# A new first stage for a hybrid decoder layer: another way to spread silu(c), sums of squares as columns, whole modulation tiles, another order of loads

## The chip, the core and the metric

The kernel runs on one core of one Trainium2 chip. Times are device microseconds of one execution. The kernel before takes 1126.01 us, the median of 3 runs (1125.87 to 1126.14).

The engines are named as in the profile: PE is TensorE (matrix products; PEld is its loading of weights), DVE is VectorE, ACT is ScalarE, SP is SyncE, which here only issues DMAs. Each engine works through its own queue in order.

## The reference

One decoder layer on 512 tokens of 1024 features. A vector c gives six modulation vectors; two of them, a shift and a scale, modulate the first norm. The normed rows h then go through one wide input projection (q, k, v, gates and the inputs of the other mixers), three mixers, an output projection, and an MLP behind a second norm.

```
cond = jax.nn.silu(c)
...
mod = (cond @ w_ada[l] + b_ada[l])[:, None, :]
sh1, sc1, g1, sh2, sc2, g2 = jnp.split(mod, 6, axis=-1)
h = _rms(x, norm1_w[l]) * (1 + sc1) + sh1
x = x + g1 * _hybrid_mixer(h, w_in[l], ...)
h = _rms(x, norm2_w[l]) * (1 + sc2) + sh2
x = x + g2 * (jnp.square(jax.nn.relu(h @ w_ff1[l])) @ w_ff2[l])
```

with `_rms(x, w) = x * rsqrt(mean(x * x) + eps) * w` over the features of a token. Everything is float32.

## The kernel before

Activations lie transposed: a block is [128 features, 512 tokens], and `xT` has eight of them. Weights are split into a high and a low part as they stream in, and a product is three fp32r matmuls (`mm3`, L284 to L287): high weight by low activation, high by high, low by high. Large products are fed by `wstream` (L274), which loads two row blocks of 512 columns into a tile `raw`, and `wsplit` (L267), which lets ACT make `wh` and DVE make `wl`. Each of the three has a pool of three buffers. Other tiles of [128, 512] come from 59 places, taken in the order in which they have been free (`Slots`).

The first stage, L330 to L486, stands in an order written out by hand for DVE, ACT, PE and SP (`manual_schedule`). It makes h and the first two chunks of the input projection, Q and K, as the modulation arrives:

- c is loaded twice in halves, spread over all 128 partitions by the DMA (L334); ACT makes silu of it in place (`crow`, L356).
- `warm(n)` (L390) is n products of 128x128 ones by ones. They feed nothing; they keep PE working. `WARM = (18, 12, 6)`.
- Squares of the eight `xT` blocks: ACT squares, DVE adds pairs (L403), and PE sums over features with a 128x128 matrix of ones (L401, L404) into `sp` [128, 512]: every partition has the sum of every token.
- DVE picks the diagonals of `sp` (L414, tile diag), so that token sums stand in a column, `ss` [128, 4]. ACT takes the square root (L416), DVE the reciprocal and one Newton step (L421 to L424).
- `diag` times ones (L428, L429) spreads 1/rms back over the partitions, tile `rp` (psrx in the profile).
- `ada_load` (L226) loads 128 rows of w_ada^T in two halves, tiles `wa`; `dot` (L362) multiplies a half by silu(c) and sums it, `dot_end` (L369) joins two halves with bias and norm weight into `A1[k]` (scale and shift of row block k).
- `high(k)` and `low(k)` (L439, L448) make the two parts `hh[k]` and `hl[k]` of h from x, 1/rms and A1; `w_load`, `w_high`, `w_low` load and split the weights of Q and K for a row block. For row block 0, `u` (L445) reads `rp` in PSUM.
- The loop of L462 runs over the eight row blocks: the loads, dots and splits of block k + 1 beside PE's 24 matmuls of block k.

Behind it a scheduler orders the work by priority; `evac` (L316) takes finished products out of PSUM, and `background` holds the other 32 modulation rows (`ada_later`, L241), one per two row blocks.

Of the kernel before, what the change touches and what calls it, by code (L numbers as in the profile page):

```python
# [17 lines left out]
P = 128  # L18
D = 1024
T = 512  # L20
# [65 lines left out]
# columns of the vector table: 128 values each  # L86
# [7 lines left out]
# chunks of 512 columns of w_in  # L94
# [4 lines left out]
def kernel(ctx: ExitStack, tc: tile.TileContext, a: dict, out: bass.AP, dbg=None):  # L99
# [16 lines left out]
    class Slots:  # L116
        """places of [128, 512] float32: the one that has been free for longest goes first"""
# [56 lines left out]
    crow = [blk("crow") for _ in range(2)]  # L174
# [8 lines left out]
    # 1/sqrt(sum/n + eps) of a small tile of sums  # L183
# [10 lines left out]
    def token_rsqrt(sums, n, name):  # L194
        """1/sqrt(sum over the partitions of sums / n + eps) on every partition, in PSUM"""
        nb = sums.shape[1] // P
        sp = psm(name)
        for b in range(nb):
            mm(sp[:, b : b + 1], lhsT=sums[:, b * P : (b + 1) * P], rhs=ones[:, 0:1], start=True, stop=True)
        ss = small([P, 4], name, 2)[:, :nb]  # L200
        V.tensor_copy(ss, sp[:, :nb])
        free(sp)
        return spread(rsqrt_small(ss, n, name + str(nb)), nb, name)

    def spread(r, nb, name):
        """columns of tokens to rows, the same on every partition, in PSUM"""
# [25 lines left out]
    def ada_dot(wa, o):  # L232
        d = small([P, 2], "dot", 4)
        for i in range(2):
            V.scalar_tensor_tensor(wa[i], wa[i], 1.0, crow[i], ALU.mult, ALU.mult, accum_out=d[:, i : i + 1])  # L235
# [12 lines left out]
    # work beside the large products: handed out one piece per two row blocks of weights  # L248
# [3 lines left out]
    def tick(n=1):  # L252
# [4 lines left out]
        if ticks[0] % 2 == 0 and background:  # L257
            background.pop(0)()
            if not background:
                free(*crow)  # L260
# [28 lines left out]
    def gemm_feat(w, nk, ch, ah, al, k0=0):  # L289
        """4 blocks [128 columns of w, 512 tokens]"""  # L290
# [10 lines left out]
    def gemm_tok(w, nk, ch, ah, al, mod, ahead=None):  # L301
        """4 blocks [128 tokens, 512 columns of w]; tokens 128 b + p, or 4 p + b with mod"""
# [13 lines left out]
    def evac(ps, name, func=AF.Copy):  # L316
        """out of PSUM, ahead of other work"""
# [13 lines left out]
    E = mybir.EngineType  # L331
    with tc.manual_schedule(engines={E.DVE, E.Activation, E.PE, E.SP}):
        for i in range(2):
            nc.sync.dma_start(crow[i], a["c"][:, i * T : (i + 1) * T].broadcast_to([P, T]))  # L334
# [6 lines left out]

        for k in range(8):
            nc.sync.dma_start(xT[k], a["x"][k])
            if k == 0:
                nc.sync.dma_start(vec, a["vec"])
            if k == 1:
                nc.sync.dma_start(cst[:, :P], a["const"][:, :P])
        wa = [ada_load(1, 0)]
        wa.append(ada_load(0, 0))
# [5 lines left out]
        for i in range(2):  # L355
            S.activation(crow[i], crow[i], AF.Silu)  # L356
        S.activation(junk1, epsc, AF.Sqrt)
        A1 = [small([P, 2], f"A1{k}") for k in range(8)]
        bsc1 = small([P, 8], "bsc1")
        dots = {}  # L360

        def dot(k, i, half):  # L362
            if (k, i) not in dots:
                dots[k, i] = small([P, 2], "dot", 4)
            x = wa[i][half]
            V.scalar_tensor_tensor(x, x, 1.0, crow[half], ALU.mult, ALU.mult, accum_out=dots[k, i][:, half : half + 1])  # L366
            free(x)

        def dot_end(k, i):  # L369
            d, o = dots[k, i], A1[k][:, i : i + 1]  # L370
            if i == 0:
                V.scalar_tensor_tensor(o, d[:, 0:1], bsc1[:, k : k + 1], d[:, 1:2], ALU.add, ALU.add)
                V.tensor_tensor(o, o, vc("norm1_w", k), ALU.mult)
            else:
                V.scalar_tensor_tensor(o, d[:, 0:1], vc("b_ada", k), d[:, 1:2], ALU.add, ALU.add)
# [18 lines left out]
        warm(WARM[0])  # L394
        sp = psm("sx")
        for k in range(0, 8, 2):
            s0, s1 = blk("sq"), blk("sq")
            S.activation(s0, xT[k], AF.Square)
            S.activation(s1, xT[k + 1], AF.Square)
            if k == 6:  # L400
                mm(sp, lhsT=ones, rhs=s0, start=False, stop=False)  # L401
            else:
                V.tensor_tensor(s1, s0, s1, ALU.add)  # L403
            mm(sp, lhsT=ones, rhs=s1, start=(k == 0), stop=(k == 6))  # L404
            free(s0, s1)
            if k == 0:
                V.tensor_scalar(bsc1, vc("b_ada", 8, 8), 1.0, None, ALU.add)
        dot(0, 0, 0)
        dot(0, 0, 1)
        dot_end(0, 0)  # L410
        ss, var, rt, r, t = (small([P, 4], "rx" + n) for n in "svryt")
        dg = [small([P, P], f"diag{b}") for b in range(4)]
        for b in range(4):
            V.scalar_tensor_tensor(dg[b], sp[:, b * P : (b + 1) * P], 1.0, ident, ALU.mult, ALU.mult, accum_out=ss[:, b : b + 1])  # L414
        free(sp)
        S.activation(rt, ss, AF.Sqrt, scale=1.0 / D, bias=epsc)  # L416
        w_high(Q, 0)
        w_high(K, 0)
        V.tensor_scalar(var, ss, 1.0 / D, EPS, ALU.mult, ALU.add)
        dot(0, 1, 0)  # L420
        V.reciprocal(r, rt)  # L421
        V.tensor_tensor(t, r, r, ALU.mult)
        V.scalar_tensor_tensor(t, t, -0.5, var, ALU.mult, ALU.mult)
        V.scalar_tensor_tensor(r, t, 1.5, r, ALU.add, ALU.mult)  # L424
        warm(WARM[1])
# [849 lines left out]
```

## Time and profile before

| | |
|---|---|
| median of 3 runs | 1126.01 us |
| the profiled execution: span | 1123.5 us |
| busy in it: PE, DVE, ACT | 1116.0, 597.9, 492.2 us |
| instructions | 14055 |
| data read from HBM | 131.41 MB, 119 GB/s over the span |

The profile has one execution. A row of its timeline is the start in us from the start of the span, the length, the engine, the line, the operation with its tiles (out<-in), its shape and xcount, and in brackets the idle time ahead of it with what ended that. Buffer numbers are left out of the tile names. A row of a table by stages is a stretch, its length, the busy time (and instructions) of PE, PEld, DVE, ACT and POOL, the granted clock of PE, the DMA share and GB/s. A grouped row ends in the busy time, the mean ns of one instruction, and the idle time ahead of the group.

### The profile page before, as it was taken

How to read it: one execution, taken by the hardware profiler on the slowest of the kernel's cores; microseconds unless marked ns; L12 is line 12 of the kernel's file. 1: busy time of each engine (PE TensorE's matmuls, PEld its weight loads, DVE VectorE, ACT ScalarE, POOL GpSimd, SP SyncE). 2: the span in 40 equal slices, each digit the busy share in tenths (PEclk: the TensorE clock that was granted, in tenths of full speed). 3: DMA queues.
4: the chain of work that ended last, by engine and by line, in shares of the span. 5: the costliest groups of instructions: out<-in, count | busy, mean ns of one | idle time of the engine just before them, and what ended most of it. 6: DMA issues, size and time to landing. Idle time of an engine off the chain costs nothing.

```text
span 1123.5 us, 14055 instructions
## 1 busy us (share of the span) xinstructions
PE 1116.0 (99%) x5414; PEld 952.2 (85%) x5414; DVE 597.9 (53%) x1210; ACT 492.2 (44%) x937; POOL 0.2 (0%) x4
## 2 busy tenths in 40 slices
PE   8999999999999999999999999999999999999998
PEld 6889998999887888888888888899888888888887
DVE  6973763572667668468833424576354233445241
ACT  5475885543497448425432123353343111344120
POOL 0000000000000000000000000000000000000000
PEclk9999999999999999999999999999999999999999
DMA  9852253333543444322333422360122233322331
GB/s 342 299 183 98 96 164 105 105 104 130 166 135 103 132 142 131 115 83 75 104 113 104 159 94 94 115 204 1 57 93 94 95 101 103 96 95 94 94 131 38
DMA packets 49347, 134.45 MB, mean 120 GB/s; under 512 B 5616, under 2 KB 6384, under 8 KB 49280
## 3 DMA queue, kind: packets, MB, share of 16 engines
q1 hardware_dynamic: 47696, 130.81, 35.6%
q10 hardware_dynamic: 1584, 2.75, 0.8%
q8 instruction: 42, 0.69, 0.2%
q14 instruction: 25, 0.20, 0.1%
HBM read 131.41 MB, written 2.13 MB: 119 GB/s over the span
## 4 chain that ended last, share of the span: by engine, by line
PE 95%; ACT 2%; DVE 2%; DMA 1%; issue 0%; SPq 0%; DVEq 0%; ACTq 0%
PE psacc L285 29%; PE psacc L287 29%; PE psacc L286 29%; PE psS L555 1%; PE psy L867 1%; PE pso L671 1%; PE psyo L875 1%; PE pso L669 1%; DVE conv L786 0%; PE pskT L539 0%; PE psqT L534 0%; PE pspT L652 0%; DVE wa L366 0%; PE psst L827 0%; DMA crow<-in_c_dram 0%; PE pssx L404 0%
## 5 line engine op out<-in xcount | busy, mean ns | idle before, releaser
L271 DVE TENSOR_TENSOR wl<-raw,wh 128x1024 fp32r<-128x1024 f32 x161 | 196.9, 1223 | 348.1 <-ACT wh L270 346.4
L270 ACT CAST wh<-raw 128x1024 fp32r<-128x1024 f32 x161 | 168.9, 1050 | 378.4 <-PE psacc L286 326.2
L285 PE MATMUL psacc<-hl,wh 128*128 128x512 f32 x416 | 168.0, 404 | 0.7 <-ACT prev L830 0.6
L287 PE MATMUL psacc<-hh,wl 128*128 128x512 f32 x416 | 163.2, 392 | 0.0
L286 PE MATMUL psacc<-hh,wh 128*128 128x512 f32 x416 | 162.1, 390 | 0.0
L285 PEld LDWEIGHTS psacc<-hl,wh 128*128 128x128 f32 x416 | 78.3, 188 | 18.0 <-issue 1.2
L287 PEld LDWEIGHTS psacc<-hh,wl 128*128 128x128 f32 x416 | 78.1, 188 | 18.2
L285 PE MATMUL psacc<-wl,hh 128*128 128x512 f32 x224 | 93.4, 419 | 0.0
L286 PEld LDWEIGHTS psacc<-hh,wh 128*128 128x128 f32 x416 | 78.2, 188 | 17.7 <-issue 1.4
L285 PE MATMUL psacc<-al,wh 128*128 128x512 f32 (+1 forms) x242 | 92.1, 381 | 0.0
L286 PE MATMUL psacc<-ah,wh 128*128 128x512 f32 (+1 forms) x242 | 92.1, 381 | 0.0
L287 PE MATMUL psacc<-ah,wl 128*128 128x512 f32 (+1 forms) x242 | 92.1, 380 | 0.0
L286 PE MATMUL psacc<-wh,hh 128*128 128x512 f32 x224 | 90.1, 402 | 0.0
L287 PE MATMUL psacc<-wh,hl 128*128 128x512 f32 x224 | 89.7, 401 | 0.0
L285 PE MATMUL psacc<-gl,wh 128*128 128x512 f32 x224 | 88.3, 394 | 0.0
L287 PE MATMUL psacc<-gh,wl 128*128 128x512 f32 x224 | 87.6, 392 | 0.0
L286 PE MATMUL psacc<-gh,wh 128*128 128x512 f32 x224 | 86.9, 388 | 0.0
L286 PEld LDWEIGHTS psacc<-wh,hh 128*128 128x128 f32 x224 | 65.9, 294 | 1.4
L285 PEld LDWEIGHTS psacc<-wl,hh 128*128 128x128 f32 x224 | 65.5, 293 | 1.7
L287 PEld LDWEIGHTS psacc<-wh,hl 128*128 128x128 f32 x224 | 65.5, 293 | 1.5
L235 DVE SCALAR_TENSOR_TENSOR wa<-wa,crow 128x512 f32<-128x512 f32 x64 | 43.5, 686 | 21.4 <-DMA wa<-in_w_ada_dram 21.3
L285 PEld LDWEIGHTS psacc<-al,wh 128*128 128x128 f32 x242 | 45.5, 188 | 8.9
(342 smaller groups left out, 1914.4 us busy)
## 6 DMA issues: line engine op xcount, KB each, us to landing
raw<-in_w_in_dram SPq DMA_DIRECT2D x80, 512.0 KB, 3.5
raw<-in_w_ff_dram SPq DMA_DIRECT2D x64, 512.0 KB, 3.5
wa<-in_w_ada_dram SPq DMA_DIRECT2D x96, 256.0 KB, 4.6
wst<-in_w_in_dram SPq DMA_DIRECT2D x16, 256.0 KB, 5.4
M<-prow SPq DMA_DIRECT2D x16, 256.0 KB, 3.4
raw<-in_w_ssd_out_dram SPq DMA_DIRECT2D x8, 512.0 KB, 3.5
raw<-in_w_pool_out_dram SPq DMA_DIRECT2D x8, 512.0 KB, 3.4
raw<-in_w_out_dram SPq DMA_DIRECT2D x8, 512.0 KB, 3.4
```

The source lines that it names most:

```text
L235: V.scalar_tensor_tensor(wa[i], wa[i], 1.0, crow[i], ALU.mult, ALU.mult, accum_out=d[:, i : i + 1])
L270: S.copy(wh, raw)
L271: V.tensor_tensor(wl, raw, wh.bitcast(F32), ALU.subtract)
L285: mm(ps, lhsT=wh, rhs=xl, start=first, stop=False)
L286: mm(ps, lhsT=wh, rhs=xh, start=False, stop=False)
L287: mm(ps, lhsT=wl, rhs=xh, start=False, stop=last)
L555: mm(so[b], lhsT=qT[:, b * P : (b + 1) * P], rhs=kT[:, (b + 1) * P - n : (b + 1) * P], start=True, stop=True)
L669: mm(od, lhsT=vs[kb][:, hs], rhs=pT[b // 2][:, cs : cs + P], start=(b == 0), stop=False, skip_group_check=True)
L671: mm(ov[:, b, :], lhsT=vs[b][:, hs], rhs=pT[0][:, b * P : (b + 1) * P], start=False, stop=(gi == 2 and b == 3), skip_group_check=True)
L867: mm(yp[half * 64 : half * 64 + 64, cs], lhsT=X[c][:, (2 * j + half) * 64 : (2 * j + half + 1) * 64], rhs=Ms[half][:, cs], start=True, sto ...
L875: mm(op[:, cs], lhsT=prev[c][:, j * P : (j + 1) * P], rhs=CT[:, cs], start=True, stop=True)
```

## The change

All of it lies in the first stage (but for `crow`, which is now one tile of its own that isn't given back, and so is read as `crow[:, i, :]` by the later dots).

- c is loaded as two rows of one partition, on ACT's DMA queue, together with the vector table and the identity. ACT makes silu of the row; PE spreads it over the partitions as a product of a row of ones with it, into two PSUM banks; DVE copies each into `crow`.
- The sums of squares: `square_sums` takes the squares as the stationary operand and one column of ones as the moving one, four products of 128x1 per call, so that token sums come out as columns. The diagonal step is gone. The last pair of squares isn't added by DVE: ACT squares one, DVE the other, and PE sums both. Behind each of the four pairs stand four `warm` products.
- A row block of w_ada is one load of 512 KB and one `dot` over 1024 elements; A1 needs one small step instead of two or one of three operands. Its tiles live in turn in the buffers of `raw`, `wh` and `wl`.
- SP's loads: the first w_ada tile goes ahead of x, the second behind it.

```diff
-    crow = [blk("crow") for _ in range(2)]
+    crow = cpool.tile([P, 2, T], F32, name="crow")
...
+        c1 = [blk("c1") for _ in range(2)]
         for i in range(2):
-            nc.sync.dma_start(crow[i], a["c"][:, i * T : (i + 1) * T].broadcast_to([P, T]))
+            nc.scalar.dma_start(c1[i][:1], a["c"][:, i * T : (i + 1) * T])
+        nc.scalar.dma_start(vec, a["vec"])
+        nc.scalar.dma_start(cst[:, :P], a["const"][:, :P])
...
+        homes = [(raws, "raw"), (wsp, "wh"), (wsp, "wl")]
+
+        def ada_whole(part, k):
+            pool, tag = homes[0]
+            homes.append(homes.pop(0))
+            w = pool.tile([P, 2, T], F32, tag=tag, name=uid("wada"))
+            nc.sync.dma_start(w, a["w_ada"][part * 8 + k].rearrange("p (i t) -> p i t", i=2))
+            return w
+
+        wa = [ada_whole(1, 0)]
         for k in range(8):
             nc.sync.dma_start(xT[k], a["x"][k])
...
-        wa = [ada_load(1, 0)]
-        wa.append(ada_load(0, 0))
+        wa.append(ada_whole(0, 0))
...
+        def dot(k, i):
+            w, o, d = wa[i], A1[k][:, i : i + 1], small([P, 1], "dot1", 4)
+            V.scalar_tensor_tensor(w, w, 1.0, crow, ALU.mult, ALU.mult, accum_out=d)
             if i == 0:
-                V.scalar_tensor_tensor(o, d[:, 0:1], bsc1[:, k : k + 1], d[:, 1:2], ALU.add, ALU.add)
-                V.tensor_tensor(o, o, vc("norm1_w", k), ALU.mult)
+                V.scalar_tensor_tensor(o, d, bsc1[:, k : k + 1], vc("norm1_w", k), ALU.add, ALU.mult)
             else:
-                V.scalar_tensor_tensor(o, d[:, 0:1], vc("b_ada", k), d[:, 1:2], ALU.add, ALU.add)
+                V.tensor_tensor(o, d, vc("b_ada", k), ALU.add)
...
         warm(WARM[0])
+        cps = [psm("c") for _ in range(2)]
+        for i in range(2):
+            S.activation(c1[i][:1], c1[i][:1], AF.Silu)
+            mm(cps[i], lhsT=ones[:1], rhs=c1[i][:1], start=True, stop=True)
+            V.tensor_copy(crow[:, i, :], cps[i])
+        free(*cps, *c1)
+        S.activation(junk1, epsc, AF.Sqrt)
+        V.tensor_scalar(bsc1, vc("b_ada", 8, 8), 1.0, None, ALU.add)
+
         sp = psm("sx")
+
+        def square_sums(s, first, last):
+            for b in range(4):
+                mm(sp[:, b : b + 1], lhsT=s[:, b * P : (b + 1) * P], rhs=ones[:, 0:1], start=first and b == 0, stop=last and b == 3, skip_group_check=True)
+
         for k in range(0, 8, 2):
             s0, s1 = blk("sq"), blk("sq")
             S.activation(s0, xT[k], AF.Square)
-            S.activation(s1, xT[k + 1], AF.Square)
-            if k == 6:
-                mm(sp, lhsT=ones, rhs=s0, start=False, stop=False)
+            if k < 6:
+                S.activation(s1, xT[k + 1], AF.Square)
+                V.tensor_tensor(s1, s0, s1, ALU.add)
             else:
-                V.tensor_tensor(s1, s0, s1, ALU.add)
-            mm(sp, lhsT=ones, rhs=s1, start=(k == 0), stop=(k == 6))
+                square_sums(s0, False, False)
+                V.tensor_tensor(s1, xT[k + 1], xT[k + 1], ALU.mult)
+            square_sums(s1, k == 0, k == 6)
             free(s0, s1)
-            if k == 0:
-                V.tensor_scalar(bsc1, vc("b_ada", 8, 8), 1.0, None, ALU.add)
-        dot(0, 0, 0)
-        dot(0, 0, 1)
-        dot_end(0, 0)
...
-        for b in range(4):
-            V.scalar_tensor_tensor(dg[b], sp[:, b * P : (b + 1) * P], 1.0, ident, ALU.mult, ALU.mult, accum_out=ss[:, b : b + 1])
...
+            warm(4)
+            if k == 2:
+                dot(0, 0)
+        dot(0, 1)
+        v, r, t, rt = (small([P, 4], "rx" + n) for n in ("v", "r", "t", "rt"))
+        S.activation(rt, sp[:, :4], AF.Sqrt, scale=1.0 / D, bias=epsc)
+        V.tensor_scalar(v, sp[:, :4], 1.0 / D, EPS, ALU.mult, ALU.add)
...
-                wa = [ada_load(1, k + 1), ada_load(0, k + 1)]
+                wa = [ada_whole(1, k + 1), ada_whole(0, k + 1)]
                 w_load(k + 1)
-                dot(k + 1, 0, 0)
+                dot(k + 1, 0)
                 if k:
                     low(k)
-                dot(k + 1, 0, 1)
                 w_high(Q, k + 1)
                 w_high(K, k + 1)
-                dot(k + 1, 1, 0)
-                dot_end(k + 1, 0)
-                dot(k + 1, 1, 1)
+                dot(k + 1, 1)
                 w_low(Q, k + 1)
-                dot_end(k + 1, 1)
```

The chain from `rt` to `diag` and `rp`, and `warm(WARM[1])` and `warm(WARM[2])` around it, stay as they were.

PE's queue from its start to the spreading of 1/rms, before (lines of the kernel before; pswarm is the tile of the warm products, pssx the sums of squares, psrx the spread 1/rms; the moving operand stands first behind the arrow):

```order
L392 MATMUL pswarm_134<-ones_87 128x128 x18
L404 MATMUL pssx_153<-sq_155,ones_87 128x512
L404 MATMUL pssx_153<-sq_162,ones_87 128x512
L404 MATMUL pssx_153<-sq_168,ones_87 128x512
L401 MATMUL pssx_153<-sq_173,ones_87 128x512
L404 MATMUL pssx_153<-sq_174,ones_87 128x512
L392 MATMUL pswarm_134<-ones_87 128x128 x12
L429 MATMUL psrx_223<-diag_49_189,ones_87 128x128
```

The same place in the changed kernel (its own line numbers; psc is silu(c) spread):

```order
L389 MATMUL pswarm_128<-ones_86 128x128 x18
L395 MATMUL psc_147<-c_15_93,ones_86 128x512
L395 MATMUL psc_148<-c_16_94,ones_86 128x512
L405 MATMUL pssx_157<-ones_86,sq_159 128x1 x4
L389 MATMUL pswarm_128<-ones_86 128x128 x4
L405 MATMUL pssx_157<-ones_86,sq_172 128x1 x4
L389 MATMUL pswarm_128<-ones_86 128x128 x4
L405 MATMUL pssx_157<-ones_86,sq_188 128x1 x4
L389 MATMUL pswarm_128<-ones_86 128x128 x4
L405 MATMUL pssx_157<-ones_86,sq_200 128x1 x4
L405 MATMUL pssx_157<-ones_86,sq_201 128x1 x4
L389 MATMUL pswarm_128<-ones_86 128x128 x16
```

The spread of c stands between the first warm products and the sums, and the warm products ahead of psrx are 16 in a row, with 12 more between the sums.

DVE's queue at the same place, before, from the first sum of squares to the first dot:

```order
L403 TENSOR_TENSOR sq_155<-sq_154,sq_155 128x512
L407 TENSOR_SCALAR bsc_32_133<-vec_76 128x8
L403 TENSOR_TENSOR sq_162<-sq_161,sq_162 128x512
L403 TENSOR_TENSOR sq_168<-sq_167,sq_168 128x512
L366 SCALAR_TENSOR_TENSOR wa_106,dot_179<-wa_106,crow_77 128x512
L366 SCALAR_TENSOR_TENSOR wa_107,dot_179<-wa_107,crow_78 128x512
```

And in the changed kernel, from the copies of `crow`:

```order
L396 COPY crow<-psc_147 128x512
L396 COPY crow<-psc_148 128x512
L399 TENSOR_SCALAR bsc_30_127<-vec_76 128x8
L412 TENSOR_TENSOR sq_159<-sq_158,sq_159 128x512
L412 TENSOR_TENSOR sq_172<-sq_171,sq_172 128x512
L368 SCALAR_TENSOR_TENSOR wada_99,dot_39_184<-wada_99,crow 128x1024
L370 SCALAR_TENSOR_TENSOR A_22_119<-dot_39_184,bsc_30_127,vec_76 128x1
L412 TENSOR_TENSOR sq_188<-sq_187,sq_188 128x512
L415 TENSOR_TENSOR sq_201<-xT_9_85 128x512
L368 SCALAR_TENSOR_TENSOR wada_109,dot_44_216<-wada_109,crow 128x1024
```

The two copies out of PSUM now stand ahead of the first sum of squares, and the first whole dot ahead of the third.

SP's queue just behind the stage in the changed kernel (raw: weights of the third chunk, two row blocks each; wa: background modulation rows); the third `raw` there stood right behind the first two `wa` before:

```order
L276 DMA raw_796<-in_w_in_dram 128x1024
L713 DMA hv_88<-in_hvec_dram 128x48
L718 DMA wdt_829<-in_w_dt_dram 128x128
L276 DMA raw_834<-in_w_in_dram 128x1024
L229 DMA wa_883<-in_w_ada_dram 128x512
L229 DMA wa_884<-in_w_ada_dram 128x512
L229 DMA wa_998<-in_w_ada_dram 128x512
L229 DMA wa_999<-in_w_ada_dram 128x512
L229 DMA wa_1149<-in_w_ada_dram 128x512
L229 DMA wa_1150<-in_w_ada_dram 128x512
L276 DMA raw_892<-in_w_in_dram 128x1024
```

The third `raw` has moved behind four more background loads.

More of the change, by code (lines that the diff above doesn't have):

```diff
@@ L234, in ada_dot @@
         for i in range(2):
-            V.scalar_tensor_tensor(wa[i], wa[i], 1.0, crow[i], ALU.mult, ALU.mult, accum_out=d[:, i : i + 1])
+            V.scalar_tensor_tensor(wa[i], wa[i], 1.0, crow[:, i, :], ALU.mult, ALU.mult, accum_out=d[:, i : i + 1])
         free(*wa)
@@ L258, in tick @@
             background.pop(0)()
-            if not background:
-                free(*crow)
     def flush():
@@ L398 @@
             S.activation(s0, xT[k], AF.Square)
[L399 to L404 removed]
+            if k < 6:
+                S.activation(s1, xT[k + 1], AF.Square)
+                V.tensor_tensor(s1, s0, s1, ALU.add)
+            else:
+                square_sums(s0, False, False)
+                V.tensor_tensor(s1, xT[k + 1], xT[k + 1], ALU.mult)
+            square_sums(s1, k == 0, k == 6)
             free(s0, s1)
[L406 to L416 removed]
+            warm(4)
[5 more added lines that the diff above has]
+        V.tensor_scalar(v, sp[:, :4], 1.0 / D, EPS, ALU.mult, ALU.add)
         w_high(Q, 0)
         w_high(K, 0)
[L419 to L420 removed]
         V.reciprocal(r, rt)
         V.tensor_tensor(t, r, r, ALU.mult)
[L423 removed]
+        V.scalar_tensor_tensor(t, t, -0.5, v, ALU.mult, ALU.mult)
         V.scalar_tensor_tensor(r, t, 1.5, r, ALU.add, ALU.mult)
+        free(sp)
         warm(WARM[1])
         rp = psm("rx")
+        dg = [small([P, P], f"diag{b}") for b in range(4)]
         for b in range(4):
@@ L431 @@
         R1 = blk("R1")
-        dot(0, 1, 1)
-        dot_end(0, 1)
         hh = [cpool.tile([P, T], F32R, name=f"hh{k}", tag=f"hh{k}") for k in range(8)]
```

15 lines of the change are left out of this document (removed).

## The prediction

> **What bounds the kernel now.** I read the page's span and busy line first, then what TensorE (PE) waited for over the whole run, then stages, and last the timeline of the first 28 us.
>
> ```profile
> span 1123.5 us, 14055 instructions
> ...
> PE 1116.0 (99%) x5414; PEld 952.2 (85%) x5414; DVE 597.9 (53%) x1210; ACT 492.2 (44%) x937; POOL 0.2 (0%) x4
> ...
> PE pssx L404 <- DVE sq L403: 1.6, 1, 1.6
> PE pswarm L392 <- DVE ones L352: 1.1, 1, 1.1
> PE psacc L285 <- ACT prev L830: 0.6, 1, 0.6
> PE psacc L287 <- DVE hl L450: 0.4, 1, 0.4
> PE psacc L285 <- ACT hh L446: 0.4, 1, 0.4
> PE psrx L429 <- DVE diag L428: 0.2, 1, 0.2
> ```
>
> The last six rows are all of PE's waits: us in total, times, longest. Five of the six lie in the first stage; behind it PE waits 0.6 us in all. So whatever the first stage loses or gains goes through to the end: nothing later has slack to swallow it, and nothing later has more than 0.6 us to give. Busy time isn't useful time, though. In the first stage PE also works through products that only keep it warm (`warm`, tile pswarm), and its queue runs in order. These rows (start, length, engine, line) are the path of that stage:
>
> ```profile
> 0.73 0.86 SPq L334 DMA_DIRECT2D crow<-in_c_dram  x2
> ...
> 1.07 6.79 PE L392 MATMUL pswarm<-ones 128*128 128x128 f32 x36 [1.07 <-DVE ones L352]
> ...
> 5.47 0.63 ACT L356 ACTIVATE crow<-crow 128x512 f32<-128x512 f32 x1 [0.33 <-DMA crow<-in_c_dram]
> 6.12 1.28 ACT L357 ACT_TABLE_LOAD   x1
> ...
> 8.69 0.69 DVE L403 TENSOR_TENSOR sq<-sq,sq 128x512 f32<-128x512 f32 x1 [2.06 <-ACT sq L399]
> ...
> 9.43 3.30 PE L404 MATMUL pssx<-sq,ones 128*128 128x512 f32 x6 [1.57 <-DVE sq L403]
> ...
> 11.30 0.63 ACT L399 ACTIVATE sq<-xT 128x512 f32<-128x512 f32 x1
> ...
> 13.43 1.02 PE L404 MATMUL pssx<-sq,ones 128*128 128x512 f32 x2
> ...
> 14.29 2.84 PE L392 MATMUL pswarm<-ones 128*128 128x128 f32 x24
> ...
> 15.45 0.30 ACT L416 ACTIVATE rxr<-rxs,epsc 128x4 f32<-128x4 f32 x1 [3.52 <-DVE diag L414]
> ...
> 16.14 0.17 DVE L421 RECIPROCAL rxy<-rxr 128x4 f32<-128x4 f32 x1
> ...
> 16.94 0.87 DVE L428 TENSOR_SCALAR diag<-cst,rxy 128x128 f32<-128x128 f32 x4
> 17.28 1.16 PE L429 MATMUL psrx<-diag,ones 128*128 128x128 f32 x8 [0.15 <-DVE diag L428]
> ...
> 18.59 0.74 DVE L445 SCALAR_TENSOR_TENSOR u<-xT,A,psrx 128x512 f32<-128x512 f32 x1
> ...
> 20.00 0.57 ACT L456 COPY R<-psrx 128x512 f32<-128x512 f32 x1
> ...
> 20.14 0.50 PE L285 MATMUL psacc<-wsl,hh 128*128 128x512 f32 x1 [0.37 <-ACT hh L446]
> ...
> 20.79 0.68 DVE L385 TENSOR_TENSOR wsl<-wst,wsh 128x512 fp32r<-128x512 f32 x1
> ...
> 24.77 0.21 DVE L375 SCALAR_TENSOR_TENSOR A<-dot,vec 128x1 f32<-128x1 f32 x1
> ...
> 24.91 0.68 DVE L443 TENSOR_TENSOR u<-u,R 128x512 f32<-128x512 f32 x1
> ...
> 26.72 0.74 DVE L450 SCALAR_TENSOR_TENSOR hl<-u,A,hh 128x512 fp32r<-128x512 f32 x1
> ...
> 27.52 0.50 PE L287 MATMUL psacc<-wsh,hl 128*128 128x512 f32 x1 [0.39 <-DVE hl L450]
> ```
>
> An f32 product is two PE passes: 18 warm products are x36. The 24 passes from 14.29 end about when the first `diag` is ready; PE waits only 0.15 us before L429. So in this kernel the filling just fits. The large products begin at 20.14 and stall once more, for the second row block's `hl`, at 27.52.
>
> **The change, by the row.** Prices first:
>
> ```profile
> 28.00:67.00 39.00, 39.00 (x169) 31.57 (x168) 38.55 (x108) 22.01 (x42) 0.00 (x0) 1.00 0.87 298
> ...
> 1.10:5.10 4.00, 4.00 (x19) 4.00 (x20) 0.00 (x0) 1.70 (x3) 0.00 (x0) 1.00 0.76 194
> ...
> 422.15 0.95 PE L199 MATMUL psrr<-ones,sums 128*128 128x1 f32 x8
> 422.95 0.48 PE L285 MATMUL psacc<-hl,wh 128*128 128x512 f32 x1
> ...
> 22.01 0.69 DVE L366 SCALAR_TENSOR_TENSOR wa<-wa,crow 128x512 f32<-128x512 f32 x1
> ...
> 22.62 0.69 DVE L366 SCALAR_TENSOR_TENSOR wa<-wa,crow 128x512 f32<-128x512 f32 x1
> ...
> L271 DVE TENSOR_TENSOR wl<-raw,wh 128x1024 fp32r<-128x1024 f32 x161 | 196.9, 1223 | 348.1 <-ACT wh L270 346.4
> ```
>
> A 512-column f32 pass: of two passes from 13.43 the next instruction starts at 14.29, so 0.43 us, and the results come 0.16 us after that (13.43 + 1.02 = 14.45). A 128-column pass, warm: 24 in 2.84 less that 0.16 is 0.112 us; the row 1.10:5.10 (a stretch, its length, PE busy and its passes) has 19 in 4.00, 0.21 each, before PE is warm. Its third number from the end, the granted clock, is 1.00 all the same: the pace, not that column, shows the difference. A one-column pass with a new 128x128 weight: the eight at 422.15 hold PE until 422.95, 0.10 each. They are exactly four products, what one `square_sums` of the change issues, in the same form. On DVE a 512-wide step comes every 0.61 us, and a 1024-wide step lasts 1.22 instead of 0.69, so every 1.15.
>
> Spread of c: the two K=1 products stand behind warm(18), whose queue lets the next start at 7.86 - 0.16 = 7.70. Four passes of 0.43: results at 8.72 and 9.58. ScalarE's silu of one row is ready well before: in the old kernel silu of c ended at 6.1 although it waited for a 256 KB broadcast. The copies out of PSUM aren't in the trace; the nearest rows are 0.69 (L403, from SBUF) and 0.74 (L445, one operand from PSUM); I take 0.69, ends 0.57 (ScalarE's copy of the same shape, L456) and 0.74. The second starts at 9.6, 0.61 later and a small step behind it the first sum of squares at 10.33, ending 11.02, against 8.69 before. This is the first loss: that sum stood behind nothing, and now stands behind two copies that wait for PE, which waits for its own filling.
>
> PE from there, in its own order: 5 `square_sums` of 0.80 are 4.00 us; 3 x 8 warm passes between them and 4 + 12 warm products = 32 passes behind the last, 56 x 0.112 = 6.27. From 11.07 that is 21.34, if PE never waits. It doesn't: the third DVE sum is ready at 13.64 (after the 1024-wide dot(0,0) at 11.55), the last square at 14.25, while PE reaches them at 14.5 and 17.0. The last sums are out at 17.93; sqrt takes 0.30, `v` behind it 0.17, and L421 to L428 0.80 as now, so `diag` runs from 19.2 to 20.1 (0.87). PE comes to it only at 21.34, through its 32 warm passes. Eight passes more, 22.24, results 22.40. So `u` of row block 0 starts at 22.42 instead of 18.59, and the first large product, 1.55 later as now, at 23.97: **+3.83 us**.
>
> What the change removes here was on the old path: ten full-width passes (10 x 0.43 = 4.3 against 4.0 now), the four `diag` reductions (from the sums at 14.45 to the sqrt at 15.45), and a half dot ahead of `u`. That saves 1.0 and 0.61 us on DVE, but DVE isn't last any more: its work hides under PE's warm passes. 256 KB x 2 of broadcast c is gone from SP's queue and the first w_ada tile has moved ahead of x; no loads are late: x7 is squared at 11.30 now, and wanted at 13.6 then. Four DMA issues on ScalarE's queue come ahead of its table load, some 1.7 us where two took SP 0.86; with a table load of 1.28 and two silus of 0.63 that is about 5.5, and silu has until 7.70.
>
> Second row block: between `u` and the `hl` that PE waits for (18.59 to 26.72, 8.13 us) the DVE now holds: 2.20 to the second `wsl` as before, 0.61 for that, dot 1.15 + 0.14 for A (24.77 to 24.91), dot 1.15 + 0.14, three steps of 0.61, the whole dot(2,0) 1.15 + 0.14 where half a dot stood: 8.51, so **+0.38 us**. Later rows: DVE needs 2 x 1.29 + 0.74 + 1.83 = 5.15 us, PE 24 passes of 0.23 (39.00 us for 169), 5.5; PE stays the bound, and DVE's smaller work is worth nothing there.
>
> Behind the stage PE's queue is the same but for neighbours that swap. The w_ada tiles now live in the buffers of `raw`, `wh`, `wl`, so the third `raw` load stands on SP behind dot(7,1) and six background loads:
>
> ```profile
> L270 ACT CAST wh<-raw 128x1024 fp32r<-128x1024 f32 x161 | 168.9, 1050 | 378.4 <-PE psacc L286 326.2
> ...
> raw<-in_w_in_dram SPq DMA_DIRECT2D x80, 512.0 KB, 3.5
> ...
> 61.66 1.99 ACT L322 COPY q<-psacc 128x512 f32<-128x512 f32 x3
> ...
> 66.36 0.40 PE L285 MATMUL psacc<-wl,hh 128*128 128x512 f32 x1
> ```
>
> dot(7,1) ends near 26.5 + 6 x 5.15 + 1.15 = 58.6; 3.5 us to land, a cast of 1.05 and a table load of 1.28 that now stands ahead of the copies: ScalarE is free for them near 64.4. Their products end at 61.66 + 4.21 = 65.9. I cost it at nothing: the cover is 1.5 us, and some 6 until PE needs the first bank, at 66.36 + 4.21.
>
> Sum: 3.83 + 0.38 = +4.2 us on the profiled span of 1123.5, which is 1127.7. The median of the runs, 1126.0, is 2.5 above that span, so **1130.2 us**.
>
> The Trainium skill, "TensorE: Matmul & The Clock Gate", section Back-to-back issue gap, puts a product of 1 to 64 columns at about 25 ns, its weights left out; by that the 40 passes would be 1.0 us instead of 4.0, and the time, an estimate, about 1127.4. Its section LDWEIGHTS has a weight load cost 128/1.2 = 107 ns however few columns follow: 4.3 us, 1130.5. The L199 row, 0.10 a pass, speaks for the second.
>
> **Rivals.**
> One-column passes that hide in the warm passes beside them (8%; the side of no loss). Taken as free, PE waits for the third sum at 13.68, ends its 32 passes 8 passes later at 18.16, `u` starts at 19.24: +0.65 + 0.38, **1127.0**. Against it: L199 measures them between full-width products, where they hid nothing. The page's 25 ns named above leads to this case. It decides from about 0.41 us a `square_sums` down (2.0 us less over five), where the whole loss falls under 2.25 us, 0.2%.
> PE falls back to its slow pace (8%): 64 passes at 0.21 instead of 0.112 add 6.3, **1136.5**, or 1140.5 if the one-column passes double too. Against it: PE idled 1.57 us before 9.43 and ran full pace after; the new gap, 9.4 to 11.07, is as long. For it: one-column work keeps little of the array busy. The Trainium skill, same page, Part 1, halves the clock after about 3.4 us idle; by that rule this gap is too short. Whether one-column passes count as work no row here shows.
> The third `raw` lands late (6%): past 68 or so ScalarE's copies hold PE's next bank, each us costs one; with 1 to 2 us, **1132**.
> Faster elsewhere (5%): the scheduler's new order takes more than the 0.6 us of later waits, and the stage loses nothing: 1123. No row points there.
>
> **Numbers.** The forecast has 73%. Its own range: one-column groups up to 0.95 instead of 0.80 (+0.75), copies -0.1 to +0.05, later waits 0.6 either way, a few tenths on the second stall: 1129.1 to 1131.8. Reaching to the free passes below and the late load above, 1126.9 to 1133.0 leaves out the slow pace, most of the faster case and a little of the rest, under 2 in 10. A measurement of this kernel can tell about 0.2%, 2.25 us, from no change: slower 0.86 (forecast, slow pace, late load, less a little), same 0.10, faster 0.04.
>
> **What would show it.** Right: PE without a gap from about 11.1 to 22.3 with the 32 warm passes starting near 17.8; DVE idle before `u` of block 0, released by psrx; first large product near 24.0; the next stall for `hl` of block 1 longer than now; behind it no new waits. Wrong: psrx waiting for `diag` (then DVE sets the end, and the one-column passes were cheap); warm passes at 0.2 us; a wait of PE at the first product of the third chunk.

## The result, and the profile after

| | before | after |
|---|---|---|
| median of the runs | 1126.08 us (4) | 1145.89 us (4) |
| the profiled execution: span | 1123.5 us | 1144.3 us |
| first large product | 20.14 us | 31.98 us |

The ratio is 1.0174, 95% interval 1.016 to 1.0188: slower, as forecast, but by 19.8 us where 4.2 were forecast, and outside the range. The page of the changed kernel (share of the span, then the granted clock in 40 slices of 28.6 us, in tenths):

```profile
span 1144.3 us, 14119 instructions
...
PE 1135.8 (99%) x5480; PEld 965.7 (84%) x5480; DVE 597.2 (52%) x1165; ACT 493.1 (43%) x937; POOL 0.2 (0%) x4
...
PEclk7999999999999999999999999999999999999999
```

PE is as full as before, so 19.8 us more of PE work, with 66 passes more in its count. The first slice has a clock of 0.7, where before it was full. The stage by tens of microseconds, in the columns of the table by stages:

```profile
10.00:20.00 10.00, 9.63 (x50) 9.63 (x50) 4.79 (x10) 1.22 (x3) 0.00 (x0) 0.57 1.02 386
20.00:30.00 10.00, 10.00 (x56) 10.00 (x54) 1.60 (x9) 1.29 (x3) 0.00 (x0) 0.58 0.99 385
```

The third number from the end is the granted clock: 0.57 and 0.58 while PE is busy for 9.63 and 10.00 of 10 us. "Busy" tells nothing of the pace. The same stretch in the timeline of the changed kernel:

```profile
6.94 1.98 PE L395 MATMUL psc<-c,ones 1*128 1x512 f32 x4
...
10.37 1.05 PE L405 MATMUL pssx<-ones,sq 128*128 128x1 f32 x8 [1.46 <-DVE sq L412]
...
11.29 1.97 PE L389 MATMUL pswarm<-ones 128*128 128x128 f32 x8
...
13.05 1.71 PE L405 MATMUL pssx<-ones,sq 128*128 128x1 f32 x8
...
23.15 6.35 PE L389 MATMUL pswarm<-ones 128*128 128x128 f32 x32
...
31.98 0.50 PE L283 MATMUL psacc<-wsl,hh 128*128 128x512 f32 x1 [0.26 <-ACT hh L452]
...
39.99 0.50 PE L285 MATMUL psacc<-wsh,hl 128*128 128x512 f32 x1 [1.17 <-DVE hl L456]
```

The first eight one-column passes still take 0.11 us each (8 in the 0.92 us from 10.37 to 11.29). From 11.29 the warm passes take 0.22 and the one-column passes 0.20: half pace, until some way into the 32 warm passes from 23.15. PE had waited 1.46 us before, less than in the old kernel.

That is 11.84 us to the first large product, and the wait for the second row block's `hl` is 1.17 instead of 0.39. But the end comes 20.8 us later, and PE's waits behind the stage don't explain the rest:

```profile
PE pssx L405 <- DVE sq L412: 1.5, 1, 1.5
PE psacc L285 <- DVE hl L456: 1.2, 1, 1.2
PE pswarm L389 <- DVE ones L360: 1.1, 1, 1.1
PE psrr L211 <- DVE diag L210: 0.6, 1, 0.6
PE psacc L283 <- DVE conv L872: 0.5, 1, 0.5
```

The products themselves do. Groups of instructions (busy time, mean ns of one), of the kernel before:

```profile
L285 PE MATMUL psacc<-hl,wh 128*128 128x512 f32 x416 | 168.0, 404 | 0.7 <-ACT prev L830 0.6
...
L287 PE MATMUL psacc<-hh,wl 128*128 128x512 f32 x416 | 163.2, 392 | 0.0
L286 PE MATMUL psacc<-hh,wh 128*128 128x512 f32 x416 | 162.1, 390 | 0.0
...
L286 PE MATMUL psacc<-ah,wh 128*128 128x512 f32 (+1 forms) x242 | 92.1, 381 | 0.0
...
L285 PE MATMUL psacc<-gl,wh 128*128 128x512 f32 x224 | 88.3, 394 | 0.0
...
L287 PE MATMUL psacc<-gh,wl 128*128 128x512 f32 x224 | 87.6, 392 | 0.0
L286 PE MATMUL psacc<-gh,wh 128*128 128x512 f32 x224 | 86.9, 388 | 0.0
```

and of the changed kernel:

```profile
L283 PE MATMUL psacc<-hl,wh 128*128 128x512 f32 x416 | 168.6, 406 | 0.8 <-DVE conv L872 0.5
L284 PE MATMUL psacc<-hh,wh 128*128 128x512 f32 x416 | 164.7, 396 | 0.0
L285 PE MATMUL psacc<-hh,wl 128*128 128x512 f32 x416 | 164.7, 396 | 0.0
...
L284 PE MATMUL psacc<-ah,wh 128*128 128x512 f32 (+1 forms) x242 | 92.2, 381 | 0.0
...
L284 PE MATMUL psacc<-gh,wh 128*128 128x512 f32 x224 | 88.6, 396 | 0.0
L283 PE MATMUL psacc<-gl,wh 128*128 128x512 f32 x224 | 88.6, 396 | 0.0
L285 PE MATMUL psacc<-gh,wl 128*128 128x512 f32 x224 | 88.5, 396 | 0.0
```

Everything with hh, hl, gh or gl as the moving operand against wh or wl is 2 to 8 ns dearer, `ah` is not. The six differences add up to 0.6 + 1.5 + 2.6 + 0.3 + 0.9 + 1.7 = 7.6 us. Nothing in the diff touches these products. What it does touch is where the tiles lie: `crow` is now one tile of 4096 bytes a partition ahead of hh, and the small tiles behind hl have other sizes. The built programs give the bytes, in a partition, from the first hh to the first wh, and the traces the mean time from the start of one pass to the next (ns):

```
                 hh to wh   modulo 2048    gh,wh   gh,wl   gl,wh
before            59,584        192        226.3   229.0   231.7
after             59,680        288        233.5   233.2   233.4
```

`ah` and `al` lie at the same place modulo 2048 as `wh` in both kernels; their full-width passes come about 227 ns apart in both.

### The profile page after: what moved, and what is told of

It reads as the page before. It is cut to its first block, busy times and chain, and to the rows that moved or that the text cites. A ratio compares the mean times of both kernels' runs of the same rounds, so it can differ in the third digit from the quotient of the medians.

```text
span 1144.3 us, 14119 instructions
## 1 busy us (share of the span) xinstructions
PE 1135.8 (99%) x5480; PEld 965.7 (84%) x5480; DVE 597.2 (52%) x1165; ACT 493.1 (43%) x937; POOL 0.2 (0%) x4
## 4 chain that ended last, share of the span: by engine, by line
PE 95%; DVE 2%; DMA 1%; ACT 0%; issue 0%; ACTq 0%; DVEq 0%
PE psacc L283 29%; PE psacc L285 28%; PE psacc L284 28%; PE pswarm L389 2%; DMA wa<-in_w_ada_dram 1%; PE psS L557 1%; PE psy L869 1%; PE pssx L405 1%; PE pso L671 1%; PE pso L673 0%; DVE wa L235 0%; PE pskT L541 0%; PE psqT L536 0%; PE psst L829 0%; PE pspT L654 0%; DVE wl L269 0%
## 5 line engine op out<-in xcount | busy, mean ns | idle before, releaser
L284 PE MATMUL psacc<-hh,wh 128*128 128x512 f32 x416 | 164.7, 396 | 0.0
```

Source lines behind the costliest of these rows:

```text
L284: mm(ps, lhsT=wh, rhs=xh, start=False, stop=False)
```

## Experiments: where the tiles lie

Theory: the place of the moving tile against the weights sets the pace of these products. Rival: it is something else in the new program, its neighbours in the queues. The edit is a hole in each partition ahead of the buffers of raw, wh, wl and the 59 places; only its size differs between the four:

```diff
+    gap = ctx.enter_context(tc.tile_pool(name="gap", bufs=1))
+    gap.tile([P, 8], F32, name="gap")
     raws = ctx.enter_context(tc.tile_pool(name="raws", bufs=3))
```

after_gap32 (8 floats). 

> The changed kernel with 32 bytes left free between the small tiles and the buffers of raw, wh, wl and the 512-wide places; nothing else differs. In the kernel before, hh lay 59,584 bytes (931 x 64) from the first wh in each partition, in the changed one 59,680 (32 more than a multiple of 64); here 59,712 (933 x 64). Placement modulo 64: the products of hh, hl, gh, gl with wh, wl go back from 233 to 229 ns apart, their rows from 396 to about 390 ns, 8 us less: 1138. Placement by the whole distance modulo 2048 (192 before, 288 after, 320 here): no gain, 1146 or a little more. Placement is nothing (the new neighbours in the queues make the products slower): 1146. The first 32 us stay as they are in each case.

after_gap1760 (440 floats). 

> The changed kernel with 1760 bytes left free at the same place, so that hh lies 61,440 = 30 x 2048 bytes from wh: the same place within a line of 2048 bytes, as the products of ah and al with wh have it in both kernels (227 ns apart in both). Placement modulo 64: 1138. Placement modulo 2048: all groups of hh, hl, gh, gl at 227 ns, about 12 us less than the changed kernel: 1134. Placement is nothing: 1146.

before_gap32, the same in the kernel before. 

> The kernel before, with 32 bytes left free at that place: hh lies 59,616 bytes from wh, 32 more than a multiple of 64 (224 modulo 2048). Placement modulo 64: it becomes as slow behind the first stage as the changed kernel, 8 us: 1134. Placement modulo 2048: a little slower, 1127 to 1130. Placement is nothing: 1126.

before_gap1856 (464 floats). 

> The kernel before, with 1856 bytes left free at that place: hh lies 30 x 2048 bytes from wh. Placement modulo 64: 1126, as it was. Placement modulo 2048: hh, hl, gh, gl with wh, wl at 227 instead of 229 ns, 1860 products, about 4 us less: 1122. Placement is nothing: 1126.

Measured, beside 1125.41 us for the kernel before on that chip (pitches as above):

```
                 median us   ratio [95%]               hh to wh   mod 2048   gh,wh   gh,wl   gl,wh
after_gap32       1146.50    1.0187 [1.0170, 1.0204]    59,712      320      233.2   233.1   233.7
after_gap1760     1134.16    1.0077 [1.0062, 1.0092]    61,440        0      226.5   226.8   227.1
before_gap32      1132.36    1.0061 [1.0046, 1.0076]    59,616      224      233.5   233.4   233.3
before_gap1856    1119.66    0.9950 [0.9934, 0.9967]    61,440        0      227.2   226.4   226.8
```

The rival is out: a hole alone costs the kernel before 7 us, or wins it 5.7. Modulo 64 is out too: 0, 192 and 320 are all multiples of 64, and the three pitches average 226.8, 229.0 and 233.3 ns there. The same place modulo 2048 gave in the changed kernel the 1134 that it was to give, and in the kernel before 2 us more than forecast. before_gap32 lost 7 us where that theory had 1 to 4, so the price doesn't grow with the distance. The groups of after_gap1760 against those of after:

```profile
L285 PE MATMUL psacc<-hl,wh 128*128 128x512 f32 x416 | 166.4, 400 | 1.1 <-DVE conv L874 0.8 <-DVE ol L313 0.2
L287 PE MATMUL psacc<-hh,wl 128*128 128x512 f32 x416 | 162.3, 390 | 0.0
L286 PE MATMUL psacc<-hh,wh 128*128 128x512 f32 x416 | 162.2, 390 | 0.0
...
L286 PE MATMUL psacc<-gh,wh 128*128 128x512 f32 x224 | 87.2, 389 | 0.0
L285 PE MATMUL psacc<-gl,wh 128*128 128x512 f32 x224 | 87.2, 389 | 0.0
L287 PE MATMUL psacc<-gh,wl 128*128 128x512 f32 x224 | 87.0, 389 | 0.0
```

2.2 + 2.4 + 2.5 + 1.4 + 1.4 + 1.5 = 11.4 us of the 11.7 gained.

ladder asks which distance counts. In before_gap1856 small holes between the eight buffers of hh move each further on:

```diff
+        for k, gap4 in enumerate((0, 8, 8, 16, 32, 64, 128, 128)):
+            if gap4:
+                cpool.tile([P, gap4], F32, name=f"gap{k}", tag=f"gap{k}")
```

> The kernel of before_gap1856 with the eight buffers of hh (and of gh, which take their places, here under the names ga to gh) set 0, 32, 64, 128, 256, 512, 1024 and 1536 bytes further on, modulo 2048, than wh and wl; hl and gl at 0. Only the same place within 2048 bytes is fast: ga with wh and wl at a mean of about 381 ns, the seven others at 388 to 396. A place modulo 512 decides: gf, gg and gh as fast as ga. Modulo 256: ge too. Nearness decides: gb and gc nearly as fast as ga, the farther ones slow. Span between 1118 and 1124.

One run, 1122.12 us. The groups of ga to gf with wh (the whole of gh has 389 in before_gap1856; the 381 of the expectation is the mean of ah's group, which mixes two forms):

```profile
L288 PE MATMUL psacc<-gc,wh 128*128 128x512 f32 x28 | 11.1, 397 | 0.0
...
L288 PE MATMUL psacc<-gb,wh 128*128 128x512 f32 x28 | 11.0, 394 | 0.0
...
L288 PE MATMUL psacc<-ge,wh 128*128 128x512 f32 x28 | 11.0, 392 | 0.0
L288 PE MATMUL psacc<-gd,wh 128*128 128x512 f32 x28 | 11.0, 391 | 0.0
...
L288 PE MATMUL psacc<-ga,wh 128*128 128x512 f32 x28 | 10.9, 390 | 0.0
...
L288 PE MATMUL psacc<-gf,wh 128*128 128x512 f32 x28 | 10.9, 389 | 0.0
```

Pitches with wh and wl: 227 to 228 for a shift of 0; 232 for 32; 235 to 236 for 64; 229 to 230 for 128; 230 and 228 for 256; 227 for 512, 1024 and 1536. So the claim "only the same place within 2048 bytes" is wrong: modulo 512 is enough, and shifts of 32 and 64 bytes cost most. The kernel could have told: the weights of one pass are 128 columns of wh or wl, 512 bytes a partition, so the four slices of a tile always stood at four places modulo 2048. It isn't this distance alone either. In the kernel before, gh,wh, gh,wl and gl,wh all lie 192 apart modulo 2048, since the buffers of hh, hl, wh and wl are multiples of 2048 bytes, and yet take 226.3, 229.0 and 231.7. And with the roles changed, wh moving and slices of hh as weights, passes still come 234 ns apart on average in before_gap1856, where the place is the same (237 to 238 in the kernel before). What in the memory does this stays open.

## Experiments: the clock of the first stage

Three things in the new stage could have let the clock fall: the one-column sums, the spread of c with one row of 128, and the idle time behind that. From here the base is after_gap1760 (first large product 31.19, span 1130.7), and each edit undoes one of them; where an edit changes the small tiles, the hole changes with it, so that hh and wh stay in the same place.

wide_sums: the sums as before, with DVE's diagonal step.

```diff
-            for b in range(4):
-                mm(sp[:, b : b + 1], lhsT=s[:, b * P : (b + 1) * P], rhs=ones[:, 0:1], ...)
+            mm(sp, lhsT=ones, rhs=s, start=first, stop=last)
```

> The kernel of after_gap1760 with the sums of squares as in the kernel before (ones as weights, 512 columns a pass, the diagonal taken out by DVE), the spread of c through TensorE and all warm products kept. One-column passes let the clock fall: granted clock 1.00 from 10 to 23 us, 128-column warm passes at 0.112 us, first large product near 24.5 instead of 31.2, span near 1124 instead of 1130.7. The spread with one row of 128, or the idle 1.45 us behind it, lets it fall: the first warm(4) still lasts about 2 us, the clock shows below 0.8 from 11 us on for some us, first large product at 27 or later, span above 1126.

full_rows: c spread with all rows, c1 zeroed ahead and loaded behind the other two loads.

```diff
-            mm(cps[i], lhsT=ones[:1], rhs=c1[i][:1], start=True, stop=True)
+            mm(cps[i], lhsT=ones, rhs=c1[i], start=True, stop=True)
```

> The kernel of after_gap1760 with c's row spread by 128 rows of ones instead of one (the other rows of c1 are zero): the same passes and columns. The one-row passes let the clock fall: now it stays at 1.00, warm passes at 0.112 us, first large product near 24, span near 1124. One-column passes or the idle time behind the spread: as after_gap1760, first large product near 31, span near 1131.

dma_c: c spread by the load, as before.

```diff
-            nc.scalar.dma_start(c1[i][:1], a["c"][:, i * T : (i + 1) * T])
+            nc.sync.dma_start(crow[:, i, :], a["c"][:, i * T : (i + 1) * T].broadcast_to([P, T]))
```

> The kernel of after_gap1760 with c spread by a broadcast load as in the kernel before, and the one-column sums kept: no passes of one row, and the first sum of squares comes about 2 us sooner. The spread's one-row passes or the wait for the copies behind them: clock 1.00, first large product near 22 to 23, span near 1122. One-column passes: the warm passes between them last 0.21 us again and the first large product comes near 29, span near 1129.

fill_gap: warm products in the idle time.

```diff
             V.tensor_copy(crow[:, i, :], cps[i])
+        warm(7)
```

> The kernel of after_gap1760 with seven more warm products in the 1.45 us in which TensorE waits between the spread of c and the first sum of squares. The idle time lets the clock fall: clock 1.00, first large product near 24, span near 1124. The one-column passes: the clock falls some us later, the first large product still comes at 28 or later, span 1128 or more. The one-row passes: as after_gap1760, 31 and 1131.

One run each: first large product and span 25.59 and 1123.2 (wide_sums), 30.68 and 1130.5 (full_rows), 31.88 and 1130.6 (dma_c), 24.19 and 1122.3 (fill_gap). The one-row passes aren't needed for the fall: full_rows and dma_c (which has no spread, and waits 2.58 us) are as slow as their base. But neither of the other two is the whole cause, since undoing either one nearly removes the loss. The clock in wide_sums:

```profile
12.00:14.00 2.00, 2.00 (x8) 1.48 (x8) 1.97 (x6) 0.00 (x0) 0.00 (x0) 0.50 1.05 416
14.00:16.00 2.00, 2.00 (x11) 1.48 (x10) 1.08 (x3) 0.00 (x0) 0.00 (x0) 0.67 1.02 400
```

It falls there too, and is back in some 3.4 us (0.67 is two thirds of 2 us at half); in the changed kernel it took some 17. So the one-column passes, 40 of PE's 64 passes from 10 to 23 us, keep the clock down, but they are not needed to start the fall. dma_c shows this too: its first one-column pass starts at 10.55, and the clock is down from 10.00 on:

```profile
8.00:10.00 2.00, 0.00 (x0) 0.00 (x0) 0.19 (x1) 1.91 (x6) 0.00 (x0) 1.00 1.06 403
10.00:12.00 2.00, 1.45 (x7) 1.45 (x7) 1.34 (x3) 1.87 (x4) 0.00 (x0) 0.50 1.04 390
```

fill_gap, with the same one-column passes and no idle time, has 1.00 in every slice.

Three more runs asked for the parts by themselves. fill_only is warm(7) in the changed kernel, buffers left where they lie. 

> The changed kernel with seven more warm products behind the spread of c and nothing else (the buffers lie as in the changed kernel). Idle time lets the clock fall and the one-column passes keep it down: granted clock 1.00 throughout, first large product near 24.2 instead of 32.0, 8 us less than the changed kernel, 1138. If the single run of fill_gap was a lucky phase of the clock: first large product at 28 or later, 1142 to 1146.

1137.25 us, ratio 1.0111 [1.0091, 1.0131], 8.6 less than the changed kernel. Its timeline:

```profile
7.54 1.98 PE L395 MATMUL psc<-c,ones 1*128 1x512 f32 x4
9.45 1.83 PE L389 MATMUL pswarm<-ones 128*128 128x128 f32 x14
11.11 0.95 PE L406 MATMUL pssx<-ones,sq 128*128 128x1 f32 x8
11.92 1.14 PE L389 MATMUL pswarm<-ones 128*128 128x128 f32 x8
...
18.18 3.82 PE L389 MATMUL pswarm<-ones 128*128 128x128 f32 x32
...
24.48 0.50 PE L283 MATMUL psacc<-wsl,hh 128*128 128x512 f32 x1 [0.25 <-ACT hh L453]
```

One-column passes at 0.10 (eight from 11.11 to 11.92), 32 warm ones in 3.65: full pace throughout, and 24.48 where the prediction had 23.97. (One of its four runs took 1141.6, with a mean granted clock of 0.997: this mixture of passes doesn't keep the clock up every time.)

thin_before puts the one-column sums into before_gap1856, without a spread; one copy of DVE stands for the diagonal step. 

> The kernel of before_gap1856 with its sums of squares taken as one-column passes (four to a product of before), the diagonal steps of DVE replaced by one copy; no spread of c through TensorE, and the idle time ahead of the first sum stays at about 1.6 us. The idle time needs only slow-filling passes behind it: the clock falls to 0.5 from 11 or 12 us on, first large product at 25 or later, span 1123 or more. It is the spread and the idle time together: the clock stays at 1.00, first large product near 20, span near 1118 as in before_gap1856.

Span 1123.0 against 1117.8, and the clock at 0.53 from 10 to 12 us:

```profile
9.62 8.26 PE L401 MATMUL pssx<-ones,sq 128*128 128x1 f32 x40 [1.59 <-DVE sq L410]
17.74 5.47 PE L394 MATMUL pswarm<-ones 128*128 128x128 f32 x24
```

40 passes in 8.1 us, 0.2 each. before_gap1856 itself waited longer, 2.25 us, ahead of full-width sums, and kept its clock in the profiled run.

wide_full has wide sums and the spread with all rows, so that idle time alone is left. 

> The kernel of wide_sums with c spread by 128 rows of ones instead of one, as in full_rows: no one-column and no one-row passes are left, the idle time behind the spread is as it was. Passes of one row keep the clock up no better than idle time: with 128 rows it stays at 1.00 from 8 to 20 us, the first large product comes about 1 us sooner than wide_sums's 25.6, span near 1122. The idle time of 1.46 us alone lets it fall, though 2.25 us did not in before_gap1856: granted clock 0.5 around 12 to 14 us as in wide_sums, first large product 25 or later, span 1123.

Span 1121.1, clock 1.00 throughout, first large product 23.61. That spoke for the one-row passes as a trigger, but one run is little, so both were run again.

> wide_sums once more, for the granted clock of each of its runs. One-row passes keep the clock up no better than idle time: its mean lies below 1.000 in every run, or all but one, and the median is near 1125. If the single fall seen in it was chance: some runs at 1.000 and near 1123, as many as in wide_full.

> wide_full once more, for the same reason. One-row passes are the cause: mean granted clock 1.000 in every run or all but one, median near 1122.9, 2 us below wide_sums. Chance: the same mixture of runs as in wide_sums, the same median.

Ten runs each, medians 1124.49 (ratio 0.9994 [0.9983, 1.0004]) and 1123.82 (0.9985 [0.9976, 0.9995]). The mean granted clock is below 1.000 in five of ten with one-row passes (0.997 or 0.998) and in none of ten without; in the kernel before itself it is 0.998 or 0.999 in 6 of 19. So "every run" was wrong, and so were the 2 us between them: the medians are 0.7 apart. Idle time like this lets the clock fall briefly in some runs, one-row passes beside it perhaps more often, though five of ten against none of ten beside 6 of 19 settles little. The changed kernel shows 0.992 to 0.994 in all four: with one-column passes behind the idle time the clock fell in each.

tuned has both remedies and less filling, to see whether the new stage can win.

```diff
-WARM = (18, 12, 6)
+WARM = (18, 6, 6)
-            warm(4)
+            if k == 2:
+                warm(3)
```

> The changed kernel with both remedies (1760 bytes left free, seven warm products behind the spread) and with fewer warm products: three behind the second sum of squares instead of four behind each, and six instead of twelve ahead of the diagonal. If PE's own queue sets the time to the first large product, that comes near 20.3, and with 1122.3 for fill_gap's span at 24.2 the span is near 1118.4 and the time near 1120, 0.5% below the kernel before. If the loads or DVE set it, the stall at the second row block grows by what the first product gains and the time stays at 1122 to 1124. If the thinner filling lets the clock fall: 1126 or more.

1122.24 us in eleven runs, ratio 0.9974 [0.9961, 0.9987]. PE never waits from 1.08 us to the first large product, and yet:

```profile
13.16 3.46 PE L408 MATMUL pssx<-ones,sq 128*128 128x1 f32 x24
16.49 2.91 PE L391 MATMUL pswarm<-ones 128*128 128x128 f32 x12
```

and by stages:

```profile
14.00:16.00 2.00, 2.00 (x16) 2.00 (x17) 1.01 (x3) 0.00 (x0) 0.00 (x0) 0.80 1.02 396
16.00:18.00 2.00, 2.00 (x10) 2.00 (x11) 0.90 (x6) 1.29 (x3) 0.00 (x0) 0.50 1.06 405
```

Here one-column passes, 40 of them with six warm ones between, brought the clock down with no idle time at all, and the first large product came at 22.70 instead of 20.3. That the median lies where late loads or DVE would have put it is chance: the wait for the second `hl` is 1.2 us, as in fill_only.

The traces hold a reading that puts all these cases together. From the clock's first rise on (4.56 to 6.94 us, different from run to run), it changes only at whole multiples of 3.41 us, in all 17 traces. What PE did in such a stretch, with a pass counted from its start to the next start, and full meaning 128 rows and at least 128 columns (us):

```
                    stretch           full   one-column   one-row   idle   clock behind it
after               7.98 to 11.39     0.10      0.91        0.94    1.46        0.50
tuned              11.77 to 15.19     0.76      2.66        0       0           0.50
after_gap32         6.94 to 10.35     1.13      0           1.98    0.30        0.50
wide_sums           8.51 to 11.92     1.29      0           0.67    1.46        0.50
dma_c               6.58 to 10.00     1.39      0           0       2.02        0.50
after_gap1760       6.32 to  9.73     1.46      0           1.96    0           1.00
wide_sums_rounds    8.89 to 12.30     1.49      0           0.47    1.46        1.00
fill_only          16.06 to 19.47     1.71      1.71        0       0           1.00
before              6.35 to  9.76     1.84      0           0       1.57        1.00
```

All eight falls in the first stage, and those at the ends of the kernels, where PE runs out of work, came behind a stretch with at most 1.39 us of full passes; no stretch with 1.41 or more had one behind it. From half pace the clock came back behind stretches with 2.83 us or more, and never with 2.63 or less. So in these traces idle time, one-column and one-row passes count alike, as time without full passes, and it depends on where the stretches happen to begin: the 2.25 us that before_gap1856 waited fell into two of them. No run was made to test this reading.

The version that beats both kernels by most is before_gap1856: the old first stage and a hole in memory.

## Why the prediction was wrong

By its own steps:

- **That the first stage's losses go through to the end** held: no wait behind it took or gave more than 0.6 us.
- **The sum on the path** held where PE keeps its pace. fill_only has 24.48 - 20.14 = +4.34 for the 3.83 forecast, and a wait of 1.2 instead of 0.39 for `hl`, +0.8 for the 0.38: 5.1 together for 4.2. The order of the terms was right too: psrx waits for PE's own warm passes, not for `diag`.
- **The prices of PE's passes** failed. "A 128-column pass, warm: ... 0.112 us" and one-column passes at 0.10 were taken for all 12 us; they hold up to the first eight one-column passes, then both double. The rival "PE falls back to its slow pace" had it, at 8%, with 1136.5 to 1140.5, and the argument against it (old idle time of 1.57 us did no harm) read the row without what stands around it: 1.84 us of full passes in the same 3.41 us there, 0.10 here. Cost: 1144.3 - 1135.8 = 8.5 us of span, 7.5 of them before the first large product; on top of the 1130.2 forecast that is 1138.7, inside this rival's bounds.
- The Trainium skill, "TensorE: Matmul & The Clock Gate", Part 1, ties the fall to about 3.4 us of idle time. The measurement differs: it fell behind 1.46 us, and in tuned behind none. Its section LDWEIGHTS gives a weight load, in ns, as its columns divided by 1.2; for 128 columns that is 107 ns, and the 0.10 us of fill_only's one-column passes, each with a new weight of 128 columns, agrees.
- **"Behind the stage PE's queue is the same but for neighbours that swap"** was given 0.6 us of later waits either way and failed. The order was no different in price, but the addresses were: 20.8 - 8.5 - 5.1 = 7.2 us by the remainder, 7.6 by the groups, and before_gap32 alone shows 7. Neither the forecast nor any rival had a term for where a tile lies.
- **The third `raw` load**, the third rival, cost nothing: no wait for it is among PE's.

Median against median: 8.5 + 7.2 + 0.9 make 16.6 us over the forecast sum; the offset of median over span was 1.6, not 2.5, and 15.7 is what the prediction missed.

## What to carry to other kernels

A pass of one column (or one row) occupies PE but does little to hold its clock: price thin passes together with everything that runs at their pace for the next 10 us, keep idle time away from them, and read the granted clock beside the busy time. In the traces of this case it was enough that about half of each 3.4 us went to full passes. A tile that is added, grown or dropped moves every tile behind it; where PE is the bound, compare the mean ns of the same products before and after, and if they differ try holes of other sizes before looking for a scheduler's fault: in the old kernel 32 bytes cost 0.6% and 1856 bytes won 0.5%. The latter is more than the new first stage brought in any version that was run (0.26%, tuned, with the hole in it).

## What the runs showed of the hardware that was not expected

- fp32r passes of 512 columns with gh or gl moving came 226 to 228 ns apart with the moving tile at the same place modulo 512 bytes as the weights, and 229 to 236 ns at most of the other distances tried (32, 64, 128, 192, 224, 256, 288, 320 bytes off; gh,wh took 226 at 192, ge,wl 228 at 256).
- The granted clock stood at 0.50 for some 17 us in which PE was never idle, 40 of its first 64 passes being one-column ones, and came back only in the dense 128-column passes from 23.15 us on. In all 17 traces it fell only behind 3.41 us with 1.39 us or less of full passes in them, idle or not.
- One-column passes with a new 128x128 weight each took 0.10 us at full clock (fill_only) and 0.20 at half. The 128-column passes beside them, which load a weight each too, took 0.11 and 0.22 to 0.23, so the columns are hardly the price. That the weight load is fits this; no run takes the load away.
